# Merging the block inverses of a gated delta rule: neighbouring matmuls on different rows of the array

## The chip, the cores and the metric

The kernel runs on one core of a Trainium2 chip, as one launch. The metric is device time in microseconds, the median of several runs. The core has five engines with instruction queues of their own: TensorE (PE; its weight loads stand in the profile as PEld), VectorE (DVE), ScalarE (ACT), GpSimd (POOL) and SyncE (SP, which issues transfers). Each works through its queue in order; semaphores tie the queues together.

## The reference

Two layers of a mixer run over a context of 256 rows and a sequence of 1024 rows, with a model width of 1024. A projection feeds a convolution branch and a branch of four heads with a gated delta rule, once forward and once backward in time. The part that the change touches solves, for every chunk of time and every head, a triangular system:

```python
lmat = jnp.where(strict, jnp.einsum('bhncd,bhnsd->bhncs', kb, k) * decay, 0.0)
eye = jnp.eye(CHUNK, dtype=jnp.float32)
rhs = jnp.concatenate([v * beta, kb * jnp.exp(g)[..., None]], axis=-1)
sol = lax.linalg.triangular_solve(eye + lmat, rhs, left_side=True, lower=True, unit_diagonal=True)
```

The solutions go into a recurrence over the chunks that carries a 128 by 128 state per head and direction. The two directions are added, normalised and gated, and a last projection with a residual closes the layer.

## The kernel before

The time axis is cut into 10 blocks of 128 rows (`NB`); the kernel's chunk is a whole block. For each head, `head_b1` computes for both directions d and all blocks the triangular matrix of keys against keys (`tt`, line 682) and its inverse, so that the recurrence (`head_rec`) needs only products. The inverse is made in three steps:

1. The four 32 by 32 diagonal blocks of every matrix are inverted on DVE by elimination, 30 steps of two instructions (lines 699 and 701), for all blocks and both directions at once. Two transposes on DVE bring the result into the forms needed as operands, `xn` (named xnat in the profile, line 705) and `xt` (xtr, line 706).
2. Pairs of 32 by 32 inverses are merged into 64 by 64 inverses: for an inverse [[A, 0], [C, D]] the missing quarter is minus D^-1 C A^-1. The first products go to the tile `pu` (line 721), ACT copies them with a minus sign to `u1` (line 729), the second products go to `py` (lines 736 and 739), and ACT copies those to their places (line 748). There are two pairs p in a block: p = 0 lies in partitions 0 to 63, p = 1 in 64 to 127. The call's `tile_position` says which rows and columns of the 128 by 128 array a matmul uses: rows start at 32 or 96 for `pu`, at 0 or 64 for `py`. Of `py` there are three kinds, called (p, "n") and (p, "t") by the operand's form; "n" and "t" of the same p use the same rows and different columns.
3. The two 64 by 64 inverses are merged in the same way into the 128 by 128 inverse, five blocks at a time: first products to `pu2` (line 754, rows 64 to 127 of the array; the prediction calls this "up"), copy to `u2` (line 759), second products to `py2` (line 764 for the forward, 767 for the backward direction, rows 0 to 63; "down"), copy into place (lines 770 and 772). In the forward direction GpSimd clears a quarter of the matrix after "up" (line 757).

`pu`, `py`, `pu2` and `py2` all take their turn in two PSUM buffers of one tag, pb, each one bank; other steps use that tag too. Outputs of p = 0 and p = 1 share a bank, in different partitions.

The order of the work as a whole comes from a plan (`PLAN`) that lists the steps of a layer (A to Z: projections of Q, K, V, Z and of the convolution, head_a, head_b1 as B, head_b2 as D, the recurrence as R, convolution taps as T, and so on), from priorities given by step (`LEAD`), and from a scheduler that sets each engine's order when the program is built. B has a priority that lets its matmuls come ahead of projections as soon as the scheduler thinks that they are ready; the projections (line 369, 24 matmuls for a segment of 256 or 512 columns) fill the pauses in between. So a change in one step may move instructions of other steps.

Of the kernel before, what the change touches and what calls it, by code (L numbers as in the profile page):

```python
# [8 lines left out]
F32 = mybir.dt.float32  # L9
# [15 lines left out]
NB = T // 128  # L25
# [45 lines left out]
def mixer_kernel(ctx: ExitStack, tc: tile.TileContext, xs, cst_d, wada, win, wab, gp_d, wout, fnw, out):  # L71
# [11 lines left out]
    def misc(shape=(128, 512)):  # L83
        return bank("pb", 2, shape)
# [306 lines left out]
    for l in range(DEPTH):  # L391
# [274 lines left out]
        def head_b1(h, kq, hs):  # L666
# [48 lines left out]
                    act.activation(aux[rs_, :, cs_], xt[rs_, NB:2 * NB, :], AF.Copy)  # L715
            for d in range(2):
                pu = misc((128, NB, 32))
                for p in range(2):
                    f_, s_ = slice(64 * p, 64 * p + 32), slice(64 * p + 32, 64 * p + 64)
                    for b in range(NB):  # L720
                        pe.matmul(pu[f_, b, :], lhsT=tt[s_, d, b, f_], rhs=xt[s_, d * NB + b, :], start=True,  # L721
                                  stop=True, tile_position=(64 * p + 32, 64 * p))
                if d == 0:
# [4 lines left out]
                    f_ = slice(64 * p, 64 * p + 32)  # L728
                    act.activation(u1[f_], pu[f_], AF.Copy, scale=-1.0)
                py = misc((128, NB, 32))  # L730
                need = ((0, "n"), (0, "t"), (1, "t")) if d == 0 else ((0, "n"), (1, "n"), (1, "t"))
                for p, w_ in need:
                    f_, s_ = slice(64 * p, 64 * p + 32), slice(64 * p + 32, 64 * p + 64)
                    for b in range(NB):
                        if w_ == "n":
                            pe.matmul(py[s_, b, :], lhsT=u1[f_, b, :], rhs=xn[f_, d * NB + b, :], start=True,
                                      stop=True, tile_position=(64 * p, 64 * p + 32))
                        else:
                            pe.matmul(py[f_, b, :], lhsT=xn[f_, d * NB + b, :], rhs=u1[f_, b, :], start=True,
                                      stop=True, tile_position=(64 * p, 64 * p))  # L740
# [5 lines left out]
                          (aux[64:96, :, 32:64], py[64:96]))  # L746
                for o_, i_ in mv:
                    act.activation(o_, i_, AF.Copy)
                for b0 in range(0, NB, 5):
                    pu2 = misc((64, 5, 64))  # L750
                    for j in range(5):
                        b = b0 + j
                        rhs = tts[0][64:128, b, 64:128] if d == 0 else aux[64:128, b, :]
                        pe.matmul(pu2[:, j, :], lhsT=tt[64:128, d, b, 0:64], rhs=rhs, start=True, stop=True,
                                  tile_position=(64, 0))
                    if d == 0:
                        pool.memset(tts[0][64:128, b0:b0 + 5, 0:64], 0.0)
                    u2 = rwp.tile([64, 5, 64], F32, tag="u1", name="u2", bufs=2)
                    act.activation(u2, pu2, AF.Copy, scale=-1.0)
                    py2 = misc((128, 5, 64))  # L760
                    for j in range(5):
                        b = b0 + j
                        if d == 0:
                            pe.matmul(py2[0:64, j, :], lhsT=aux[0:64, b, :], rhs=u2[:, j, :], start=True, stop=True,
                                      tile_position=(0, 0))
                        else:
                            pe.matmul(py2[64:128, j, :], lhsT=u2[:, j, :], rhs=tts[1][0:64, b, 0:64], start=True,
                                      stop=True, tile_position=(0, 64))
                    if d == 0:
                        act.activation(tts[0][0:64, b0:b0 + 5, 64:128], py2[0:64], AF.Copy)  # L770
                    else:
                        act.activation(tts[1][64:128, b0:b0 + 5, 0:64], py2[64:128], AF.Copy)
            return tts

        def head_b2(h, kq, v, hs):
# [317 lines left out]
```

## Time and profile before

| What | us |
|---|---|
| median of 3 runs | 1629.67 |
| lowest and highest run | 1625.31, 1635.13 |
| profiled execution, own time | 1630.59 |
| its span, first to last instruction | 1628.9 |
| PE busy | 1498.2 |
| DVE busy | 1264.7 |
| ACT busy | 896.5 |
| POOL busy | 147.0 |

The busy time of an engine is the time in which at least one of its instructions was under way. Matmuls are pipelined, so a record of 0.19 us does not mean that the next one starts 0.19 us later: what a group of matmuls costs is read from the start of its first to the start of the next work. A matmul in 4-byte numbers leaves two weight loads and two matmul records. In the timeline neighbouring records of the same kind are merged into one row with a count, and the row's length runs to the end of its last record.

### The profile page before, as it was taken

How to read it: one execution, taken by the hardware profiler on the slowest of the kernel's cores; microseconds unless marked ns; L12 is line 12 of the kernel's file. 1: busy time of each engine (PE TensorE's matmuls, PEld its weight loads, DVE VectorE, ACT ScalarE, POOL GpSimd, SP SyncE). 2: the span in 40 equal slices, each digit the busy share in tenths (PEclk: the TensorE clock that was granted, in tenths of full speed). 3: DMA queues.
4: the chain of work that ended last, by engine and by line, in shares of the span. 5: the costliest groups of instructions: out<-in, count | busy, mean ns of one | idle time of the engine just before them, and what ended most of it. 6: DMA issues, size and time to landing. Idle time of an engine off the chain costs nothing. (4 is left out here: it accounts for less than half of the span.)

```text
span 1628.9 us, 27580 instructions
## 1 busy us (share of the span) xinstructions
PE 1498.2 (92%) x10536; PEld 1029.2 (63%) x10536; DVE 1264.7 (78%) x2813; ACT 896.5 (55%) x2009; POOL 147.0 (9%) x252
## 2 busy tenths in 40 slices
PE   7898899899999998999799999898999999999697
PEld 1564576478556765676577664675575575577576
DVE  3867889988596978876587578889898887877475
ACT  3756466466537563654443465684675666476221
POOL 0002001100111011101000010011011001111000
PEclk9798999999999999999899999999999999999899
DMA  9212102410232123333653131014013201253541
GB/s 303 96 51 104 40 28 82 155 40 27 72 114 91 53 94 98 112 134 131 218 162 113 40 96 60 28 59 133 19 45 118 84 27 72 92 173 106 188 157 70
DMA packets 83264, 158.21 MB, mean 97 GB/s; under 512 B 5606, under 2 KB 52700, under 8 KB 83132
## 3 DMA queue, kind: packets, MB, share of 16 engines
q1 hardware_dynamic: 67344, 96.74, 19.2%
q0 software_dynamic: 15280, 59.52, 10.4%
q8 instruction: 83, 1.36, 0.3%
q14 instruction: 49, 0.40, 0.1%
q10 hardware_dynamic: 508, 0.19, 0.0%
HBM read 125.43 MB, written 30.99 MB: 96 GB/s over the span
## 5 line engine op out<-in xcount | busy, mean ns | idle before, releaser
L369 PE MATMUL pj<-hhi,whi 128*128 128x512 f16 (+1 forms) x1184 | 427.8, 361 | 7.9 <-ACT whi L292 5.3
L369 PE MATMUL pj<-hhi,wlo 128*128 128x512 f16 (+1 forms) x1184 | 428.5, 362 | 2.9 <-DVE wlo L293 2.6
L369 PE MATMUL pj<-hlo,whi 128*128 128x512 f16 (+1 forms) x1184 | 428.2, 362 | 0.0
L369 PEld LDWEIGHTS <-whi 128*128 128x128 f16 x2368 | 233.5, 100 | 183.2 <-issue 18.8
L531 DVE SCALAR_TENSOR_TENSOR acc<-u,cws,acc 128x960 f32<-128x960 f32 (+26 forms) x240 | 228.3, 951 | 2.7 <-ACT acc L514 1.1
L369 PEld LDWEIGHTS <-wlo 128*128 128x128 f16 x1184 | 118.2, 100 | 91.9 <-issue 8.1
L966 PE MATMUL pj<-woh,yh 128*128 128x512 f32 x256 | 102.6, 401 | 9.7 <-ACT yh L959 9.7
L616 DVE SCALAR_TENSOR_TENSOR kq<-raw,cst,kq 128x1284 f32<-128x1284 f32 (+1 forms) x64 | 94.6, 1479 | 14.3 <-ACT kq L614 14.1
L966 PE MATMUL pj<-woh,yl 128*128 128x512 f32 x256 | 101.5, 398 | 4.6 <-DVE yl L960 4.6
L284 ACT ACTIVATE whi<-wst 128x1024 bf16<-128x1024 f32 x56 | 59.1, 1056 | 80.3 <-PE pj L369 72.7
L966 PE MATMUL pj<-wol,yh 128*128 128x512 f32 x256 | 101.8, 398 | 0.0
L833 ACT ACTIVATE vs<-rc,hs 128x128 f32<-128x128 f32 x144 | 52.4, 368 | 66.4 <-PE rc L830 64.5
L699 DVE TENSOR_TENSOR et<-xp 128x30 f32<-128x30 f32 (+14 forms) x240 | 83.8, 349 | 5.7
L701 DVE TENSOR_TENSOR xp<-xp,et 128x30 f32<-128x30 f32 (+14 forms) x240 | 80.6, 336 | 5.5
L292 ACT ACTIVATE whi<-wst,w_s 128x1024 f16<-128x1024 f32 x56 | 64.3, 1148 | 36.9 <-DVE w_s L152 36.0
L293 DVE SCALAR_TENSOR_TENSOR wlo<-wst,w_s,whi 128x1024 f16<-128x1024 f32 x56 | 73.9, 1320 | 12.6 <-ACT whi L292 12.6
L162 PE MATMUL pw<-scond,wst 128*128 128x128 f32 x512 | 68.6, 276 | 0.3 <-DVE md L179 0.3
L162 PEld LDWEIGHTS pw<-scond,wst 128*128 128x128 f32 x512 | 63.0, 191 | 3.4 <-DVE md L179 1.2
L840 PE MATMUL rc<-vs,ktm 128*128 128x128 f32 x288 | 61.7, 301 | 3.7 <-ACT vn L836 3.0
L840 PEld LDWEIGHTS rc<-vs,ktm 128*128 128x128 f32 x288 | 43.8, 190 | 30.3 <-ACT vn L836 25.4
L966 PEld LDWEIGHTS pj<-woh,yh 128*128 128x128 f32 x256 | 49.1, 192 | 20.5 <-ACT yh L959 9.9
L589 ACT ACTIVATE raw<-pj,wm 128x512 f32<-128x512 f32 (+1 forms) x68 | 42.2, 621 | 33.4 <-PE pj L369 24.1
(365 smaller groups left out, 3021.5 us busy)
## 6 DMA issues: line engine op xcount, KB each, us to landing
wst<-in_win_dram SPq DMA_DIRECT2D x56, 512.0 KB, 3.6
row<-rdr POOLq DMA_DIRECT2D x35, 640.0 KB, 4.8
wst<-in_wada_dram SPq DMA_DIRECT2D x32, 512.0 KB, 3.6
x<-in_xs_dram SPq DMA_DIRECT2D x20, 512.0 KB, 7.0
ast<-in_wada_dram SPq DMA_DIRECT2D x8, 1024.0 KB, 10.8
wst<-in_wout_dram SPq DMA_DIRECT2D x16, 512.0 KB, 4.2
y<-ydr SPq DMA_DIRECT2D x18, 448.0 KB, 6.8
a<-cdr SPq DMA_DIRECT2D x9, 512.0 KB
```

Source lines behind the costliest of these rows:

```text
L162: pe.matmul(o, lhsT=w[:, k, :], rhs=scond[:, k:k + 1, :].to_broadcast([128, 64, 2]), start=(k == 0), stop=(k == KT - 1))
L284: act.activation(hi.bitcast(BF16), st, AF.Square, accum_out=ss)
L292: act.activation(hi, st, AF.Identity, scale=s[:, 0:1])
L293: dve.scalar_tensor_tensor(out=lo, in0=st, scalar=s[:, 0:1], in1=hi, op0=MUL, op1=SUB)
L369: pe.matmul(pj[:, 0:n], lhsT=a[:, k, :], rhs=b[:, k, t0:t0 + n], start=(i == 0), stop=(i == 3 * KT - 1))
L531: gates["big"] = dve.scalar_tensor_tensor(out=ao, in0=ui, scalar=cws[:, 0, j:j + 1], in1=ao, op0=MUL, op1=ADD)
L616: gates["big"] = dve.scalar_tensor_tensor(out=dst, in0=src[:, o0 + j:o0 + j + n], scalar=col("sw", j0 + j), in1=dst, op0=MUL, op1=ADD)
L699: dve.tensor_tensor(out=ev, in0=xp[:, j + 1:, j:j + 1].to_broadcast([128, ni, j]), in1=xp[:, j:j + 1, 0:j].to_broadcast([128, ni, j]), op=MUL)
L701: dve.tensor_tensor(out=xp[:, j + 1:, 0:j], in0=xp[:, j + 1:, 0:j], in1=ev, op=ADD)
L833: act.activation(vss[d], pns[d], AF.Identity, scale=hs[:, 2 + d, bs[d]:bs[d] + 1])
L840: pe.matmul(pkv, lhsT=ktm[:, bs[d], :], rhs=vss[d], start=True, stop=True)
L966: pe.matmul(pj[hf], lhsT=a[:, k, :], rhs=w[k][:, hf * 512:(hf + 1) * 512], start=k == 0 and i == 0, stop=k == KT - 1 and i == 2)
```

## The change

`head_b1` issues the same matmuls on the same operands in another order. In `pu` the two pairs p alternate block by block, where all blocks of p = 0 came ahead of all of p = 1. In `py` the three kinds alternate block by block, in an order that puts different rows next to each other. In the last merge the "down" of the first five blocks alternates with the "up" of the other five, and the two copies at the end follow both "down" groups; the tiles `pu2` of the second five and `py2` of the first five are taken ahead of that group. The new local functions `up`, `down` and `turn` stand in the diff.

```diff
--- before.py
+++ after.py
@@ -715,9 +715,10 @@
                     act.activation(aux[rs_, :, cs_], xt[rs_, NB:2 * NB, :], AF.Copy)
             for d in range(2):
                 pu = misc((128, NB, 32))
-                for p in range(2):
-                    f_, s_ = slice(64 * p, 64 * p + 32), slice(64 * p + 32, 64 * p + 64)
-                    for b in range(NB):
+
+                for b in range(NB):
+                    for p in range(2):
+                        f_, s_ = slice(64 * p, 64 * p + 32), slice(64 * p + 32, 64 * p + 64)
                         pe.matmul(pu[f_, b, :], lhsT=tt[s_, d, b, f_], rhs=xt[s_, d * NB + b, :], start=True,
                                   stop=True, tile_position=(64 * p + 32, 64 * p))
                 if d == 0:
@@ -728,10 +729,10 @@
                     f_ = slice(64 * p, 64 * p + 32)
                     act.activation(u1[f_], pu[f_], AF.Copy, scale=-1.0)
                 py = misc((128, NB, 32))
-                need = ((0, "n"), (0, "t"), (1, "t")) if d == 0 else ((0, "n"), (1, "n"), (1, "t"))
-                for p, w_ in need:
-                    f_, s_ = slice(64 * p, 64 * p + 32), slice(64 * p + 32, 64 * p + 64)
-                    for b in range(NB):
+                need = ((0, "n"), (1, "t"), (0, "t")) if d == 0 else ((1, "n"), (0, "n"), (1, "t"))
+                for b in range(NB):
+                    for p, w_ in need:
+                        f_, s_ = slice(64 * p, 64 * p + 32), slice(64 * p + 32, 64 * p + 64)
                         if w_ == "n":
                             pe.matmul(py[s_, b, :], lhsT=u1[f_, b, :], rhs=xn[f_, d * NB + b, :], start=True,
                                       stop=True, tile_position=(64 * p, 64 * p + 32))
@@ -746,30 +747,48 @@
                           (aux[64:96, :, 32:64], py[64:96]))
                 for o_, i_ in mv:
                     act.activation(o_, i_, AF.Copy)
-                for b0 in range(0, NB, 5):
-                    pu2 = misc((64, 5, 64))
-                    for j in range(5):
-                        b = b0 + j
-                        rhs = tts[0][64:128, b, 64:128] if d == 0 else aux[64:128, b, :]
-                        pe.matmul(pu2[:, j, :], lhsT=tt[64:128, d, b, 0:64], rhs=rhs, start=True, stop=True,
-                                  tile_position=(64, 0))
+                u2, pu2, py2 = {}, {}, {}
+
+                def up(b0, j):
+                    b = b0 + j
+                    rhs = tts[0][64:128, b, 64:128] if d == 0 else aux[64:128, b, :]
+                    pe.matmul(pu2[b0][:, j, :], lhsT=tt[64:128, d, b, 0:64], rhs=rhs, start=True, stop=True,
+                              tile_position=(64, 0))
+
+                def down(b0, j):
+                    b = b0 + j
+                    if d == 0:
+                        pe.matmul(py2[b0][0:64, j, :], lhsT=aux[0:64, b, :], rhs=u2[b0][:, j, :], start=True, stop=True,
+                                  tile_position=(0, 0))
+                    else:
+                        pe.matmul(py2[b0][64:128, j, :], lhsT=u2[b0][:, j, :], rhs=tts[1][0:64, b, 0:64], start=True,
+                                  stop=True, tile_position=(0, 64))
+
+                def turn(b0):
                     if d == 0:
                         pool.memset(tts[0][64:128, b0:b0 + 5, 0:64], 0.0)
-                    u2 = rwp.tile([64, 5, 64], F32, tag="u1", name="u2", bufs=2)
-                    act.activation(u2, pu2, AF.Copy, scale=-1.0)
-                    py2 = misc((128, 5, 64))
-                    for j in range(5):
-                        b = b0 + j
-                        if d == 0:
-                            pe.matmul(py2[0:64, j, :], lhsT=aux[0:64, b, :], rhs=u2[:, j, :], start=True, stop=True,
-                                      tile_position=(0, 0))
-                        else:
-                            pe.matmul(py2[64:128, j, :], lhsT=u2[:, j, :], rhs=tts[1][0:64, b, 0:64], start=True,
-                                      stop=True, tile_position=(0, 64))
+                    u2[b0] = rwp.tile([64, 5, 64], F32, tag="u1", name="u2", bufs=2)
+                    act.activation(u2[b0], pu2[b0], AF.Copy, scale=-1.0)
+
+                pu2[0] = misc((64, 5, 64))
+                for j in range(5):
+                    up(0, j)
+                turn(0)
+
+                pu2[5], py2[0] = misc((64, 5, 64)), misc((128, 5, 64))
+                for j in range(5):
+                    down(0, j)
+                    up(5, j)
+                turn(5)
+                py2[5] = misc((128, 5, 64))
+                for j in range(5):
+                    down(5, j)
+                for b0 in (0, 5):
+                    py2_ = py2[b0]
                     if d == 0:
-                        act.activation(tts[0][0:64, b0:b0 + 5, 64:128], py2[0:64], AF.Copy)
+                        act.activation(tts[0][0:64, b0:b0 + 5, 64:128], py2_[0:64], AF.Copy)
                     else:
-                        act.activation(tts[1][64:128, b0:b0 + 5, 0:64], py2[64:128], AF.Copy)
+                        act.activation(tts[1][64:128, b0:b0 + 5, 0:64], py2_[64:128], AF.Copy)
             return tts
 
         def head_b2(h, kq, v, hs):
```

What the scheduler makes of it is shown at three places of PE's order.

The first is on PE in the first head, forward direction, at the second products `py` (pb in the rows; u is the copied first product, xnat one form of the 32 by 32 inverses; whi, wlo, hhi and hlo belong to a projection). Before:

```order
L369 LDWEIGHTS whi
L369 MATMUL pj<-hlo,whi 128x512
L736 MATMUL pb<-xnat,u_1849 32x32 x10
L739 MATMUL pb<-u_1849,xnat 32x32 x20
L369 LDWEIGHTS wlo
L369 MATMUL pj<-hhi,wlo 128x512
```

and with the change:

```order
L369 MATMUL pj<-hlo,whi 128x512
L737 MATMUL pb<-xnat,u_1849 32x32
L369 LDWEIGHTS wlo
L369 MATMUL pj<-hhi,wlo 128x512
L369 LDWEIGHTS whi
L369 MATMUL pj<-hhi,whi 128x512
L740 MATMUL pb<-u_1849,xnat 32x32 x2
L737 MATMUL pb<-xnat,u_1849 32x32
L740 MATMUL pb<-u_1849,xnat 32x32 x2
L737 MATMUL pb<-xnat,u_1849 32x32
```

The thirty matmuls alternate now, and two matmuls of a projection have come between the first and the rest.

The second is on PE in the same head and direction, in the last merge, where "down" of the first five blocks (L764, then L761) meets "up" of the other five (L754, then L755). Before:

```order
L369 LDWEIGHTS whi
L369 MATMUL pj<-hlo,whi 128x512
L764 MATMUL pb<-u_1893,aux 64x64 x5
L754 MATMUL pb<-tt 64x64 x5
L369 LDWEIGHTS wlo
```

and with the change:

```order
L761 MATMUL pb<-u_1893,aux 64x64
L755 MATMUL pb<-tt 64x64
L761 MATMUL pb<-u_1893,aux 64x64
L755 MATMUL pb<-tt 64x64
L761 MATMUL pb<-u_1893,aux 64x64
L755 MATMUL pb<-tt 64x64
L761 MATMUL pb<-u_1893,aux 64x64
L755 MATMUL pb<-tt 64x64
L761 MATMUL pb<-u_1893,aux 64x64
L755 MATMUL pb<-tt 64x64
```

The two groups of five, next to each other already, alternate matmul by matmul.

The third is on PE ahead of the second head's first products (L721, then L722), with the numbers of the tiles, since the rows read alike without; pj_3348 is a segment of a convolution projection with the weights 2713, pj_3321 and pj_3375 are segments of another with the weights 3183. Before:

```order
L369 LDWEIGHTS wlo_2755
L369 MATMUL pj_3348<-hhi_82,wlo_2755 128x512
L369 LDWEIGHTS whi_3183
L369 MATMUL pj_3375<-hhi_82,whi_3183 128x512
L721 MATMUL pb_3000<-xtr_2985,tt_2864 32x32 x20
L369 LDWEIGHTS whi_3183
```

and with the change:

```order
L369 MATMUL pj_3321<-hhi_82,whi_3183 128x512
L369 LDWEIGHTS whi_3183
L369 MATMUL pj_3321<-hlo_83,whi_3183 128x512
L369 LDWEIGHTS wlo_3190
L369 MATMUL pj_3321<-hhi_82,wlo_3190 128x512
L369 LDWEIGHTS whi_2713
L369 MATMUL pj_3348<-hhi_82,whi_2713 128x512
L722 MATMUL pb_3000<-xtr_2985,tt_2864 32x32 x20
```

The segment pj_3348 had been finished ahead of that group and is only begun there now.

## Rows read from the trace of the kernel before

**Rows 1.** The page's head: span, then busy time of each engine.

```profile
span 1628.9 us, 27580 instructions
...
PE 1498.2 (92%) x10536; PEld 1029.2 (63%) x10536; DVE 1264.7 (78%) x2813; ACT 896.5 (55%) x2009; POOL 147.0 (9%) x252
```

**Rows 2.** Table by stretches, columns: stretch, length, busy us of PE, PEld, DVE, ACT, POOL.

```profile
327.00:470.00 143.00, 137.87 (x1093) 98.03 (x1093) 111.40 (x229) 80.89 (x190) 7.82 (x14) 0.98 0.17 56
...
1277.00:1405.50 128.50, 121.72 (x918) 78.79 (x919) 108.59 (x230) 78.77 (x180) 9.09 (x15) 0.99 0.16 56
```

**Rows 3.** Chain that ended last, 1277 to 1310, shares by engine and line.

```profile
by line: PE pj L369 40.7%; PE pb L721 8.7%; PE pb L783 8.2%; PE pb L754 8.1%; PE pa L167 6.8%; PE pw L162 6.6%; PE pb L736 5.6%; DVE xtr L706 5.4%; PE pb L739 5.3%; PE pb L767 4.3%; PE pb L764 4.0%; PE pb L803 1.0%; issue 0.4%; PE pw L290 0
```

**Rows 4.** The same chain, 1373 to 1405.

```profile
by line: DVE et L699 27.8%; DVE xp L701 25.9%; issue 14.6%; DVE xp L694 6.3%; DVE xtr L706 5.9%; DVE wlo L293 4.0%; DVE sgz L596 4.0%; ACT xg L689 2.3%; DVE u L502 2.2%; PE pj L369 1.4%; DVE wm L298 1.2%; DVE ost L142 1.0%; PE pa L876 0.8%;
```

**Rows 5.** Waits of PE: us in total, times, longest.

```profile
PE pb L721 <- DVE xtr L706: 22.3, 7, 4.4
...
PE pb L721 <- DVE ost L872: 2.7, 1, 2.7
```

**Rows 6.** Timeline of PE at 181: start, us, engine, line, instruction, count, idle.

```profile
181.00 1.35 PE L721 MATMUL pb<-xtr,tt 32*32 32x32 f32 x40 [3.33 <-DVE xtr L706]
182.28 0.39 PE L369 MATMUL pj<-hlo,whi 128*128 128x256 f16 x1
```

**Rows 7.** Timeline of PE at 188, second products, first direction of the first head.

```profile
187.92 0.72 PE L736 MATMUL pb<-xnat,u 32*32 32x32 f32 x17
188.46 0.21 PE L739 MATMUL pb<-u,xnat 32*32 32x32 f32 x1
188.48 0.19 PE L736 MATMUL pb<-xnat,u 32*32 32x32 f32 x1
188.51 0.19 PE L739 MATMUL pb<-u,xnat 32*32 32x32 f32 x1
...
189.74 0.39 PE L369 MATMUL pj<-hhi,wlo 128*128 128x512 f16 x1
```

**Rows 8.** Timeline of PE at 191 to 194, the 64 by 64 groups.

```profile
191.29 0.76 PE L754 MATMUL pb<-tt 64*64 64x64 f32 x10
191.99 0.39 PE L369 MATMUL pj<-hhi,wlo 128*128 128x512 f16 x1
192.21 0.38 PE L369 MATMUL pj<-hhi,whi 128*128 128x512 f16 x1
...
192.83 0.62 PE L764 MATMUL pb<-u,aux 64*64 64x64 f32 x7
193.24 0.27 PE L754 MATMUL pb<-tt 64*64 64x64 f32 x1
...
193.96 0.39 PE L369 MATMUL pj<-hhi,wlo 128*128 128x512 f16 x1
```

**Rows 9.** Timeline of PE at 71, gate projection.

```profile
71.34 0.17 PE L431 MATMUL pb<-gw,hlo 128*128 128x16 f16 x1
...
71.59 0.18 PE L429 MATMUL pb<-gw,hhi 128*128 128x32 f16 x1
```

**Rows 10.** Timeline of PE at 344 to 346, second head, other direction.

```profile
344.15 0.81 PE L736 MATMUL pb<-xnat,u 32*32 32x32 f32 x20
344.90 0.28 PE L369 MATMUL pj<-hlo,whi 128*128 128x256 f16 x1
345.11 0.72 PE L736 MATMUL pb<-xnat,u 32*32 32x32 f32 x17
...
346.39 0.28 PE L369 MATMUL pj<-hhi,wlo 128*128 128x256 f16 x1
```

**Rows 11.** Timeline of ACT at 1284.

```profile
1284.74 0.43 ACT L748 ACTIVATE aux<-pb 32x320 f32<-32x320 f32 x1 [3.10 <-PE pb L739]
```

**Rows 12.** Timeline of PE at 327, second head.

```profile
326.94 2.15 PE L721 MATMUL pb<-xtr,tt 32*32 32x32 f32 x40 [4.21 <-DVE xtr L706]
329.03 0.61 PE L369 MATMUL pj<-hlo,whi 128*128 128x512 f16 x1
```

## The prediction

> **What bounds the kernel now.** I read the page first: TensorE (PE) is busy 1498.2 us of 1628.9, VectorE (DVE) 1264.7 us [rows 1]. Neither is idle for long, so the next view is the table by stretches, cut where the first merge group of each head starts (8 heads: 4 in each of 2 layers). In two such stretches PE is busy 137.87 of 143 us and 121.72 of 128.5; DVE 111.40 and 108.59 [rows 2]. So PE is nearly full, and DVE is the second bound.
>
> The chain shows how they alternate. From 1277 to 1310, the merges of one head, it runs on PE almost alone [rows 3]; the other items there are projections that fill the pauses between merge groups. From 1373 to 1405, the elimination of the next head, it runs on DVE, and ends with the transpose `xtr` [rows 4]. PE then waits for that transpose before the first merge group: 22.3 us in 7 heads, and 2.7 us in the eighth for another DVE instruction [rows 5]. A microsecond saved on PE in a merge is thus on the path where it is saved, but a head later the elimination on DVE may take it back. PE's total alone does not tell the gain.
>
> **What a merge group costs now.** A matmul in 4-byte numbers leaves two records, called passes here. All of it repeats in both directions of 8 heads, 16 times.
>
> - First products, `pu`: 20 matmuls, 40 passes. The group starts at 181.00 and the next work at 182.28: 1.28 us [rows 6].
> - Second products, `py`: 30 matmuls, 60 passes, from 187.92 to 189.74: 1.81 us [rows 7]. The first 17 passes take 0.72 us, of which the last alone lasts 0.19; with a longer first step that is 32 to 33 ns from start to start.
> - 64 by 64, "up": 5 matmuls, 10 passes, 191.29 to 191.99: 0.70 us, and 58 to 60 ns from start to start ((0.76-0.22)/9 = 60) [rows 8].
> - 64 by 64, "down" of the first five blocks and "up" of the other five, one behind the other: 192.83 to 193.96, 1.13 us [rows 8].
>
> What two tiles of the array do at once can be seen where one run of matmuls hands over to the next. At 188.46 a pass of L739 starts while four of L736 are still to come or just begun, and for 0.1 us both lines start a pass every 32 ns, each at its own pace: 188.46 and 188.51 for L739, 188.48 between them for L736 [rows 7]. At 193.24 the same happens between L764 (rows 0 to 63 of the array) and L754 (rows 64 to 127) [rows 8]. So matmuls on different tiles do overlap and the second does not slow the first; in the order of before it lasts for a few passes only, since the next row group is ten or twenty passes away.
>
> **The change, part by part.** (1) Alternating `pu`. Without any other limit, two streams of 20 passes would need 20 times 32 ns, 0.64 us. But PE has to be handed the instructions too. The densest stretch of the trace that lasts is the gate projection: from 71.34 to 71.59 ten matmuls, each with its weight load, start 25 ns apart, with 16 and with 32 columns alike [rows 9]. The handover at 188.46 is denser, but there the passes were already queued. The two bounds for a pass are therefore 16 ns (the handover's pace) and 25 ns; above them stands 32 ns, no gain. I take 25: it is the only pace here that holds over many matmuls, although with other operands. Then `pu` takes 39 x 0.025 + 0.12 (the time from its last start to the next work, 182.28 - 181.00 - 1.16) = 1.10 us: 0.18 saved. At 16 ns it would be 0.50.
>
> (2) `py` by the same pace: 59 x 0.025 = 1.48 us between first and last start, where it was 1.81 - 0.12 = 1.69: 0.21 saved. Its three products lie on three tiles, two of them on the same rows; the handover from L736 to L739 at 188.46 was between just those two, so same rows with other columns do not exclude overlap. If all three ran abreast, 60 passes would need 20 x 32 = 0.64 us: 1.03 saved (0.65 to stay on the safe side of first-pass delays).
>
> (3) Middle 64 by 64 group: at 58 ns a pass the 25 ns floor does not bind. Ten passes of each stream side by side take what one takes alone, 0.70 us, plus a few hundredths: 0.75 against 1.13, 0.38 saved. The lone "up" at the start and "down" at the end stay as they are.
>
> (4) Splits. In the forward direction the second matmul of `py` now needs the second half of `u1`, which ScalarE (ACT) copies last. The order answers with a split: one matmul, a few projections, then the other 29. There are seven such splits where there was one. The trace has one: 344.15 to 344.90 and 345.11 to 346.39, 0.75 + 1.28 = 2.03 against 1.81 us for a whole group, 0.22 each [rows 10]. Six more cost 1.3 us.
>
> (5) ACT's copies. They might have started on the half that was ready first, and interleaving makes all halves ready last. But in the trace they start only when the whole group is over: the first copy of `py` at 1284.74 after a wait of 3.10 us for L739, though its operand comes from the first run, L736 [rows 11]. So nothing is lost there, and a shorter group lets them start earlier. GpSimd's (POOL's) clears of the merged quarters wait for the same groups as before; PSUM buffers turn over in the same order, with two in use at a time.
>
> (6) A projection changes places. Between the first groups of the first and the second head the order has 387 projection matmuls in 16 bits before and 363 after: 24 of them, one segment of a convolution projection, now come behind the second head's first group. At their pace of 0.22 us (191.99, 192.21) [rows 8] that is 5.2 us. PE already waits 4.21 us in front of that group [rows 12], so it arrives earlier for nothing, and the stretch behind it, where PE is busy 137.87 of 143 us, gets 5.2 us more; its end has 2.7 us of PE waiting [rows 5] to take up a part. I count 2.5 us lost; bounds 0 and 5.2. DVE's set of instructions between these points does not change by more than a few short ones.
>
> **The sum.** PE saves 16 x (0.18 + 0.21 + 0.38) = 12.3 us, less 1.3 for splits: 11.0. Of this I let 60% arrive: in the stretch from 1277 to 1405.5 the merge and its tail (33 us) are PE's, the last 32 us are DVE's, and DVE is busy 108.59 of 128.5 us. 6.6 us gained, less 2.5 for the moved projection: 4.1. The profiled execution took 1630.59 us, its span 1628.9; the median of the three runs, 1629.67, is within 0.1% of it. 1630.6 - 4.1 = 1626.5, rounded to **1626**.
>
> A rule of the Trainium skill speaks against parts 1 and 2. TensorEngine Tiling (Array Packing), "Restrictions and Gotchas", says that different row tiles cannot access the same PSUM bank at the same time; `pu` and `py` each lie in one bank. By that rule only the middle group, whose two outputs lie in two buffers, would gain. The trace disagrees where it can: 60 passes of `py` at 32 ns would take 1.92 us between first and last start, and with two handovers they take 1.69, so both overlap, the one between two row groups as well as the one between two column groups.
>
> **The rivals.** *No floor at 25 ns.* For it: the handover's pace. Against it: it never lasts. Then PE saves 16 x (0.50 + 0.65 to 1.03 + 0.38) = 24 to 31 us, less 1.3; 60% of it is 14 to 18, less 2.5: about **1617**, down to 1615. The Trainium skill's page "TensorE: Matmul & The Clock Gate", Part 3, "The mechanism", shows matmuls on different row groups starting some 4 ns apart, which would be this case; no stretch of this trace holds such a pace.
>
> *Alternation does not pay in the 32 by 32 groups* (each change of tile costs what the overlap gives, or one bank serves one row group). Then 16 x 0.38 - 1.3 = 4.8, 60% of it 2.9, less 2.5: **1630**, no change.
>
> *Slower: the elimination swallows it.* PE reaches each first group earlier, DVE does not, and PE only waits longer. The price is the moved segment in full, 5.2 us, and a slower PE behind longer waits: after 4.21 us of idling the second head's first group takes 329.03 - 326.94 = 2.09 us where the first head's takes 1.28 [rows 6, 12], about what the lower of the clock's two levels, 1.2 and 2.4 GHz, makes of it. One such loss of 0.8 us more in three heads, 2.5, with 1.3 for splits: 1630.6 + 5.2 + 2.5 + 1.3 = **1639.6**. It decides if the transposes `xtr` come no earlier than before, counted from the merge ahead of them.
>
> **How the numbers follow.** Forecast (25 ns, partly arriving) 0.50; no floor 0.22; no gain in the small groups 0.15; swallowed 0.13. The order moves many other instructions by a few places, which I take as some 6 us either way around each case. A measurement of this kernel tells about 0.5%, 8 us, from no change. Faster by more: most of the second case (0.19) and about a third of the first (0.16): 0.35. Slower by more: 0.07 of the last case, 0.03 from the scatter of the first and 0.02 from the third: 0.12. The rest, 0.53, is within 0.5%. The range of 8 in 10 runs from the no-floor case to just short of the swallowed one: 1612 to 1638.
>
> **What would show it.** In the profile of the changed kernel: neighbours in `pu` 25 ns apart and the group 1.10 us (0.7 without a floor, 1.28 without overlap); `py` about 1.6 us to the next work; the middle group 0.75 us; PE's wait for `xtr` grown from 22.3 us by several us, above all at the second head. If the groups shrink as said and the time does not move, part 6 and the elimination took it; if they shrink to half, the floor was wrong; if the whole gets slower with short groups, the moved order is the cause.

## The result and the profile after

The changed kernel takes 1611.32 us (median of four runs, 1609.66 to 1614.86) beside 1629.87 for the kernel before (1625.31 to 1635.13): a ratio of 0.9875, 95% interval 0.9845 to 0.9904, about 20 us faster. (The medians lie 18.6 us apart. Ratios, and the gains in us taken from them below, are not quotients of medians; the two differ by up to some 2 us.) That is just below the low end of the predicted range (1612) and 15 us below the predicted time. The profiled execution took 1614.86 us.

The page's head, as in [rows 1]:

```profile
span 1612.9 us, 27598 instructions
...
PE 1471.7 (91%) x10536; PEld 998.6 (62%) x10536; DVE 1265.0 (78%) x2813; ACT 897.5 (56%) x2009; POOL 144.4 (9%) x252
```

The same matmuls keep PE busy 26.5 us less; DVE and ACT did not change. The timeline of PE at the first head, as in [rows 6] (start, us, engine, line, instruction, count, idle before):

```profile
182.22 0.82 PE L722 MATMUL pb<-xtr,tt 32*32 32x32 f32 x40 [3.33 <-DVE xtr L706]
182.97 0.28 PE L369 MATMUL pj<-hlo,whi 128*128 128x256 f16 x1
```

The group `pu` goes from 1.28 to 0.75 us. In `py` of the other direction, the counterpart of [rows 7], all three kinds run abreast:

```profile
198.12 0.22 PE L737 MATMUL pb<-xnat,u 32*32 32x32 f32 x2
198.13 0.21 PE L740 MATMUL pb<-u,xnat 32*32 32x32 f32 x1
198.17 0.20 PE L737 MATMUL pb<-xnat,u 32*32 32x32 f32 x2
198.18 0.19 PE L740 MATMUL pb<-u,xnat 32*32 32x32 f32 x1
...
198.75 0.19 PE L740 MATMUL pb<-u,xnat 32*32 32x32 f32 x1
198.88 0.39 PE L369 MATMUL pj<-hlo,whi 128*128 128x512 f16 x1
```

Sixty passes start between 198.12 and 198.75, 10.7 ns apart on the mean (0.63/59), in rounds of three every 32 ns; the group takes 0.76 us where [rows 7] has 1.81. The middle 64 by 64 group, as in [rows 8], "down" and "up" in pairs:

```profile
201.84 0.27 PE L764 MATMUL pb<-tt,u 64*64 64x64 f32 x1
201.84 0.27 PE L755 MATMUL pb<-aux,tt 64*64 64x64 f32 x1
201.94 0.22 PE L764 MATMUL pb<-tt,u 64*64 64x64 f32 x1
201.95 0.22 PE L755 MATMUL pb<-aux,tt 64*64 64x64 f32 x1
...
202.57 0.39 PE L369 MATMUL pj<-hlo,whi 128*128 128x512 f16 x1
```

It takes 0.73 us, was 1.13 (in two of the sixteen such groups 0.94 and 1.09). Waits of PE (us in total, times, longest), as in [rows 5]:

```profile
PE pb L722 <- DVE xtr L706: 20.8, 7, 4.6
...
PE rc L872 <- DVE row L816: 3.0, 1, 3.0
PE pb L722 <- DVE ost L891: 2.7, 1, 2.7
```

The wait for the transposes did not grow (25.0 us before, 23.5 after, with the one for ost); a wait of 3.0 for L816 is new.

**One measure for all runs.** For every merge group of a trace I take the time from its first start to the start of the next work on PE, and add them up. Before: 96.1 us. After: 63.0. So the merges give PE 33.1 us back, three times the 11.0 of the prediction's sum. That is more than by the rows above, since groups at the lower clock, which take twice as long, shrink too, and in these traces three first groups instead of four lie at it as a whole (granted clock 0.50).

### The profile page after: what moved, and what is told of

It reads as the page before. It is cut to its first block, busy times and chain, and to the rows that moved or that the text cites. A ratio compares the mean times of both kernels' runs of the same rounds, so it can differ in the third digit from the quotient of the medians.

```text
span 1612.9 us, 27598 instructions
## 1 busy us (share of the span) xinstructions
PE 1471.7 (91%) x10536; PEld 998.6 (62%) x10536; DVE 1265.0 (78%) x2813; ACT 897.5 (56%) x2009; POOL 144.4 (9%) x252
## 5 line engine op out<-in xcount | busy, mean ns | idle before, releaser
L369 PE MATMUL pj<-hhi,whi 128*128 128x512 f16 (+1 forms) x1184 | 427.0, 361 | 11.1 <-DVE sgz L596 5.2
L369 PE MATMUL pj<-hhi,wlo 128*128 128x512 f16 (+1 forms) x1184 | 425.7, 360 | 3.8 <-DVE wlo L293 3.8
L369 PE MATMUL pj<-hlo,whi 128*128 128x512 f16 (+1 forms) x1184 | 427.1, 361 | 0.0
L369 PEld LDWEIGHTS <-whi 128*128 128x128 f16 x2368 | 232.3, 100 | 187.0 <-issue 22.8
L369 PEld LDWEIGHTS <-wlo 128*128 128x128 f16 x1184 | 118.1, 100 | 93.1 <-DVE wlo L293 7.6
L845 DVE SCALAR_TENSOR_TENSOR bv<-rc,hs,bv 128x128 f32<-128x128 f32 x144 | 48.1, 347 | 18.2 <-PE rc L844 15.4
```

The source lines that it names most:

```text
L369: pe.matmul(pj[:, 0:n], lhsT=a[:, k, :], rhs=b[:, k, t0:t0 + n], start=(i == 0), stop=(i == 3 * KT - 1))
```

## The experiments

Two questions. First, what is the pace of matmuls on different tiles: does each tile keep its own (theory), or can PE start none sooner than 25 ns after the last (the prediction's choice)? Second, 33 us less on PE gave 20 us: does a fixed share arrive, or does all of it arrive and the new order of the other engines' work cost something (theory O)? Each run stands against the kernel before on the same chip.

### One edit at a time, in the order of before

Only `pu` by turns; the order of all other engines' instructions is that of before.

```diff
-                for p in range(2):
-                    f_, s_ = slice(64 * p, 64 * p + 32), slice(64 * p + 32, 64 * p + 64)
-                    for b in range(NB):
+                for b in range(NB):
+                    for p in range(2):
+                        f_, s_ = slice(64 * p, 64 * p + 32), slice(64 * p + 32, 64 * p + 64)
                         pe.matmul(pu[f_, b, :], ...
```

> The kernel before with one part of the change alone: the first products pu alternate between the two pairs. Every engine's order outside these groups is word for word that of the kernel before. Theory 'overlap': the group takes 0.75 us as in the changed kernel and not 1.28 (1.2 and not 2.1 where the clock is low), PE saves 16 x 0.53 = 8.5 us or a little more, and somewhat over half of it arrives, as of the whole change (18.6 of 33): 1624 to 1626, ratio 0.996 to 0.998. Rival 'order' (the new order of the other instructions brings the gain): groups shorter, time as before, ratio 0.999 to 1.001.

Measured: 0.992 (0.9898 to 0.9941), 13 us faster. The merge groups take 87.0 us, 9.1 less: 0.57 per group, not 0.18. The rival is out; the theory's own ratio (0.996 at best) lies outside the interval too, for more time came than PE was freed of.

In the second run `pu` is as before, and in `py` the two kinds of one pair, which use the same rows and different columns, alternate:

```diff
-                for p, w_ in need:
+                pairs = (((0, "n"), (0, "t")), ((1, "t"),)) if d == 0 else (((0, "n"),), ((1, "n"), (1, "t")))
+                for p, w_, b in [(p, w_, b) for pr in pairs for b in range(NB) for p, w_ in pr]:
```

> The kernel before with another part alone, in a form that keeps the order of all other engines: in the second products py only the two kinds on the same rows and different columns alternate, the third kind stays a run by itself. Theory 'any two tiles overlap': the group of 60 passes falls from 1.81 to about 1.3 us (two runs of 20 at 32 ns), PE saves 16 x 0.5 = 8 us, ratio 0.995 to 0.998. Rival 'only different rows overlap': the group stays at 1.8 us, ratio 0.999 to 1.001.

Measured: 0.9929 (0.9905 to 0.9952), 12 us faster; merge groups 87.5 us, 8.6 less. Its timeline of PE:

```profile
187.72 0.21 PE L737 MATMUL pb<-xnat,u 32*32 32x32 f32 x1
187.72 0.21 PE L740 MATMUL pb<-u,xnat 32*32 32x32 f32 x1
187.77 0.19 PE L737 MATMUL pb<-xnat,u 32*32 32x32 f32 x1
187.78 0.19 PE L740 MATMUL pb<-u,xnat 32*32 32x32 f32 x1
```

Behind the first pass both kinds start every 32 ns, up to 10 ns apart, and the group takes 1.29 us (187.72 to the next work at 189.00). Different columns are enough for two matmuls to overlap; the rows need not differ.

### The new order without the overlap

The order of the changed kernel on the other engines, but within the merge groups runs of one tile again:

```diff
-                for b in range(NB):
-                    for p in range(2):
+                for p in range(2):
+                    for b in range(NB):
...
+                turns = [(0, w) for w in need] + [(b, w) for w in need for b in range(1, NB)]
...
+                for f, b0, j in ((down, 0, 0), (down, 0, 1), (down, 0, 2), (down, 0, 3), (up, 5, 0), ...
```

> The changed kernel with its own order on all other engines, kept word for word, but inside the merge groups runs of the same tile: pu by pairs, py by kinds after the first matmul of each kind, the middle group in runs of four. Theory 'overlap': the groups are nearly as long as before (pu 1.28, py 1.7 to 1.8, middle 0.9 to 1.0 us), PE loses some 27 of the 33 us again, and the time goes back to 1624 to 1632. Rival 'order': the time stays at 1610 to 1616.

Measured: 1.0008 (0.999 to 1.0026). The new order alone brings nothing in sum, and the rival 'order' is out. The merge groups still took 90.8 us, 5.3 less, from the handovers that are left; that these 5.3 us did not show in the time is the first sign that the new order costs something.

### The pace by itself

Matmuls of 32 by 32 between two other steps, each kind in a loop of its own (r is the first row of the tile in the array, the next argument its first column, the last says 16 bits), written to a PSUM tile that nobody reads; the rest is the changed kernel.

```diff
+                pe.matmul(**one(o, j, 0, 0, False))
+            for j in range(16):
+                for r in (0, 32):
+                    pe.matmul(**one(o, j, r, r + 32, False))
...
+                for r in (0, 32, 64, 96):
+                    pe.matmul(**one(o, j, r, r, True))
```

> The changed kernel with test matmuls of 32 by 32 put in once behind the gate values of the first layer: in 4 bytes 16 on one tile, 32 on two tiles of different rows, 32 on two tiles of the same rows, 64 on four tiles; in 16 bits 16 on one tile and 64 on four tiles. Theory 'each tile its own pace, no floor': 32, 16, 16 and 8 ns from pass to pass; in 16 bits below 25 ns on one tile. Rival 'a matmul can be handed over every 10.6 ns at best', the pace of py in the changed kernel: 32, 16, 16 and 10.6. If the 25 ns of the gate projection are a floor for matmuls with 16-bit operands, both patterns of these stand at 25.

Timeline of PE, lines 491 (one tile), 498 (two tiles, same rows), 502 (four tiles), 505 and 509 (16 bits: one tile, four tiles); then a table of two stretches with the granted clock in the third column from the right:

```profile
90.87 1.10 PE L491 MATMUL pb<-gg 32*32 32x32 f32 x29
...
93.82 1.92 PE L498 MATMUL pb<-gg 32*32 32x32 f32 x64
95.67 0.61 PE L369 MATMUL pj<-hhi,wlo 128*128 128x512 f16 x1
96.21 1.71 PE L502 MATMUL pb<-gg 32*32 32x32 f32 x110
...
98.47 0.50 PE L505 MATMUL pb<-hhi,gw 32*32 32x32 f16 x13
...
98.85 0.70 PE L509 MATMUL pb<-hhi,gw 32*32 32x32 f16 x60
```

```profile
90.90:92.30 1.40, 1.40 (x65) 1.40 (x66) 1.40 (x3) 0.00 (x0) 0.00 (x0) 1.00 0.72 257
92.40:99.50 7.10, 6.84 (x313) 5.67 (x307) 2.83 (x7) 0.87 (x4) 0.00 (x0) 0.50 0.02 5
```

One tile at the full clock, 2.4 GHz: (1.10 - 0.19)/28 = 32.5 ns a pass. From 92.4 on the granted clock is 0.50, the level of 1.2 GHz, so the later lines are slow in themselves; even so two tiles on the same rows take (1.92 - 0.24)/63 = 27 ns a pass, and four tiles (1.71 - 0.24)/109 = 13.5 ns (what is taken off is the length of one pass). In 16 bits one tile takes (0.50 - 0.18)/12 = 27 ns, four tiles (0.70 - 0.18)/59 = 8.8 ns a pass. At this clock neither the 8 ns that the theory expected of four tiles in 4 bytes nor less than 25 ns on one tile in 16 bits could be seen, and no run shows them at the full clock. But 8.8 ns rules out both the floor of 25 ns and the rival's 10.6. So the 25 ns of [rows 9] cannot have been the pace at which PE is handed instructions. They would fit the pace of one stretch of array that every matmul there uses, as one tile in 16 bits takes 27 ns here; at the full clock that was not tried.

### Adding up in the order of before

The first two edits together; the order of the other engines is that of before.

> pu by turns and, in py, the two kinds of one pair (same rows, other columns) by turns, as the two runs before did one at a time; the order of DVE, ACT, POOL and SP is that of before, instruction for instruction. The merge groups should occupy PE 96.1 - 9.1 - 8.6 = 78.4 us. Theory O (overlap is worth more than 100% of what it takes off PE, and the new order of the changed kernel costs part of it): the two gains add up, 12.4 + 11.5 = 24 us, ratio 0.985, no worse than the changed kernel, which takes 33 us off PE instead of 18. Theory S (about 56% of any PE time saved arrives, and the two single gains were generous by chance): 17.7 x 0.56 = 10 us, ratio 0.994.

Measured: 0.9887 (0.9866 to 0.9907), 18.5 us (15.2 to 21.9) for 17.4 us of PE (groups 78.7). In sum all of it arrives: half of the changed kernel's PE gain brings nearly its whole time gain. Both theories' numbers miss the interval, 0.994 (S) by far and 0.985 (O), for the two single gains did not add up in full.

Then "down" and "up" overlap by two blocks as well, with the copy of the first half ahead of the second "down":

```diff
+                for j in range(3):
+                    down(0, j)
+                for j in range(2):
+                    down(0, 3 + j)
+                    up(5, j)
+                for j in range(3):
+                    up(5, 2 + j)
+                evac(0)
```

> As the run before it, and down of the first five blocks overlaps up of the second five by two blocks, with the copy of the first half straight behind; the order of the other engines then differs from before in a few places only (60 rows of DVE against 1138 in the changed kernel). Theory O: as the run before it and about 3 us less, ratio 0.983. Theory S: 12 us, 0.993. If the early copies or the wait for the second down lose, it is above the run before it.

Measured: 0.9875 (0.9848 to 0.9902), 20.4 us for 19.7 us of PE. From the run before it the intervals cannot tell it apart; 0.993 (S) and 0.983 (O) both lie outside.

The changed kernel beside them:

> The changed kernel on this chip, beside the others: 0.9875 by its own measurement (0.9845 to 0.9904). Both theories expect that; it is there to set the others against.

Measured: 0.9855 (0.9831 to 0.9879), 23.7 us for 33.0 us of PE (groups 63.1).

The last run here has `pu` by turns and all three kinds of `py` by turns, without the change to the 64 by 64 groups; its scheduler result is a third order:

```diff
-                for p, w_ in need:
+                turns = [(p, w_, b) for b in range(NB) for p, w_ in need]
+                for p, w_, b in turns:
```

> pu by turns and py's three kinds by turns, one pass of each, in the order of the kinds that before has; the 64x64 group stays as before. Only these; the other engines' order then moves of itself, at other places than in the changed kernel (1152 rows of DVE differ from it). PE occupation about 96.1 - 9.1 - 17 = 70 us. Theory S: 26 x 0.56 = 14.6 us, 0.991. Theory O: the overlap alone is worth up to 30 us (0.982), minus what this third order costs or plus what it gains; if it comes out near e5 though it saves 8 us more on PE, the order decides over the rest.

Measured: 0.99 (0.9876 to 0.9924), 16.3 us for 21.8 us of PE (groups 74.3). It frees 4.4 us more of PE than the fifth run (e5 in the expectation) and is no faster, so time does not follow PE's gain alone. It does not decide between the theories: S named 0.991, O left open what a third order costs. In its trace the stretch behind the last head's first merges is the longest of all, 130.1 us against 117.7 in the fifth run.

### Mixing the orders by head

Where does the changed kernel's order cost time? Cut by heads' first merge groups, its trace was longer than that of the fifth run in two places: from the first to the third head (285.8 and 288.2 us in its two traces above, against 283.2), where a projection segment was moved, and behind the last head's first merges (124.3 and 123.2 against 117.7). The form of the fifth run keeps the order of before, head by head, so it can be put in just there:

```diff
+FULL = [(0, 2), (0, 3), (1, 0), (1, 1), (1, 2)]
...
+                full = (l, h) in FULL
+                if full:
+                    need = ((0, "n"), (1, "t"), (0, "t")) if d == 0 else ((1, "n"), (0, "n"), (1, "t"))
+                    pairs = (need,)
+                else:
+                    pairs = (((0, "n"), (0, "t")), ((1, "t"),)) if d == 0 else (((0, "n"),), ((1, "n"), (1, "t")))
...
+                if not full:
+                    for b0 in range(0, NB, 5):
...
+                    continue
```

> The changed kernel, but three of the eight heads (the first two of the first layer and the last of the second) have pu by turns, py's two kinds of one pair by turns and the 64x64 group as before, which gives these heads the order of before on the other engines; the remaining five have the changed code and the changed order. By theory O (the new order costs time in just these places) the stretches should be those of the run with that form in the first two heads (283 us from the first to the third head's merges, against 286 to 288 in the changed kernel) and in the last (118 against 123 to 124), and those of the changed kernel elsewhere: 8 to 10 us less than the changed kernel, about 1602, ratio 0.981. Rival F (the order does not matter, PE time saved does): three heads give back 2 us of PE each, 56% of it arrives: 3 us slower than the changed kernel, 0.988.

Measured: 0.9823 (0.9799 to 0.9848), median 1603.45 us: 28.9 us for 29.2 us of PE. It is the fastest, 7.5 us below the changed kernel on the same chip (1610.96), although PE has 3.9 us more to do in the merges. Rival F is out, and the two stretches came out as expected, 283.3 and 117.7 us.

But the new order does not only cost. Between the first merges of the third and of the fifth head all traces do the same 3489 matmuls (give or take two at the edges). Here are that stretch before, in the fifth run (overlap, order of before), in the third (new order, little overlap) and in this one (stretch, length, busy us of PE, PEld, DVE, ACT, POOL, granted clock, DMA share, GB/s):

```profile
470.00:1023.60 553.60, 515.28 (x3489) 364.45 (x3489) 418.28 (x997) 293.63 (x651) 55.18 (x90) 0.97 0.34 108
```

```profile
464.50:1018.20 553.70, 517.89 (x3489) 365.86 (x3489) 420.16 (x997) 293.40 (x651) 55.77 (x90) 0.96 0.33 108
```

```profile
475.30:1018.50 543.20, 512.74 (x3489) 362.51 (x3489) 417.69 (x998) 294.06 (x652) 53.41 (x90) 0.98 0.33 110
```

```profile
464.20:1006.80 542.60, 506.22 (x3489) 355.46 (x3489) 417.79 (x997) 294.03 (x651) 53.62 (x90) 0.98 0.34 111
```

In all five traces with the order of before it takes 553.6 to 555.6 us, in all eight with the changed order 542.6 to 545.9. So the new order is worth some 10 us there, and the overlap nothing in either order. One part of it is a wait of PE for ACT's copy to `aux` between the third and the fourth head, 3.9 us before (start, us, engine, line, instruction, count, idle; the granted clock is 0.51 in the group behind it) and 4.9 in the fifth run:

```profile
496.23 1.32 PE L754 MATMUL pb<-aux,tt 64*64 64x64 f32 x10 [3.89 <-ACT aux L748]
```

In the third run it is gone; the rest of the 10 us I have not traced. That 28.9 us arrived for 29.2 is therefore partly chance: some 10 of them are the order's.

In the last head alone:

> The changed kernel with that smaller form in the last head of the second layer alone; the order of DVE is that of the changed kernel up to that head's transposes and that of before behind them. Theory O: the tail has 118 us instead of 123 to 124, PE's wait of 3 us for the row work in it is gone: 1605 to 1606, ratio 0.983. Rival F: 1 us slower than the changed kernel, 0.987. Rival P (the tail's length hangs on the moment at which it starts, not on its order): anything between.

Measured: 0.9847 (0.9823 to 0.9872), median 1605.99, 5.0 us below the changed kernel. The two intervals overlap, and rival F's 0.987 lies just inside this one, so the time alone does not settle it; the traces say more. The tail, first of the changed kernel, then of this run (columns as above):

```profile
1385.00:1509.20 124.20, 107.88 (x862) 73.43 (x862) 87.74 (x194) 75.72 (x174) 16.25 (x27) 0.94 0.36 123
```

```profile
1382.50:1499.40 116.90, 104.82 (x862) 74.06 (x862) 86.70 (x194) 74.36 (x174) 16.46 (x27) 0.97 0.39 131
```

The same number of matmuls, 7.3 us shorter: PE is busy 3.1 us less, with the clock at 0.97 instead of 0.94, and idle 4.2 us less. (Against the changed kernel's trace on this chip, 122.2 us at a clock of 0.96, it is 5.3 us shorter.) The place is the recurrence of that head. In the changed kernel PE stands still for 3 us there, and just behind it the granted clock falls to 0.50 (from 1423.2 to 1426.5), a projection starting every 0.43 us instead of 0.22:

```profile
1419.16 0.39 PE L873 MATMUL rc<-na,vn 128*128 128x128 f32 x2
1422.53 0.49 PE L872 MATMUL rc<-row,S 128*128 128x128 f32 x2 [2.99 <-DVE row L816]
...
1424.69 0.63 PE L369 MATMUL pj<-hhi,wlo 128*128 128x512 f16 x1
1425.12 0.63 PE L369 MATMUL pj<-hhi,whi 128*128 128x512 f16 x1
```

In this run (L369, 872 and 873 are here L371, 905 and 906) projections lie at that place:

```profile
1417.43 0.39 PE L906 MATMUL rc<-na,vn 128*128 128x128 f32 x2
1417.66 0.38 PE L371 MATMUL pj<-hlo,whi 128*128 128x512 f16 x1
...
1420.46 0.38 PE L371 MATMUL pj<-hhi,wlo 128*128 128x512 f16 x1
1420.68 0.38 PE L905 MATMUL rc<-row,S 128*128 128x128 f32 x2
```

The traces of the other runs agree. The wait of 3 us for L816 or its counterpart stands in all six traces with the changed order in the last head and in no other. With that order the tail takes 122.2 to 124.3 us in five traces and 126.1 without the overlap; with the order of before it takes 116.9 to 118.6 in five traces with some overlap and 119.8 without. One trace does not fit: in that of the sixth run, whose DVE order there is that of before, it has 124.2 us, with a wait of PE of 2.1 us for another step. It is by far the slowest execution of that run (1622.69 us, the others 1607.62 to 1612.44), so the order of DVE does not fix the tail in every execution.

The first two heads alone:

> The changed kernel with the smaller form in the first two heads of the first layer alone; that puts the 24 projection matmuls back behind the first head's merges (387 and 407 of them in the first two stretches, where the changed kernel has 363 and 431). Part 6 of the prediction: the moved segment costs 2.5 us (0 to 5.2), of which the smaller overlap gives back 4 us of PE, 2.3 of time: no change against the changed kernel or up to 3 us faster, 0.984 to 0.986. If the move cost nothing, 2.3 us slower than it, 0.987 to 0.988.

Measured: 0.986 (0.9836 to 0.9883), median 1609.61: 1.4 us below the changed kernel, within what was expected for a segment that costs 2.5 us, but too little to be told from no effect. The stretch itself is clearer; the changed kernel first, then this run:

```profile
182.20:468.00 285.80, 266.01 (x2155) 183.38 (x2156) 244.11 (x491) 166.92 (x399) 23.70 (x37) 0.98 0.21 67
```

```profile
179.00:463.00 284.00, 266.71 (x2156) 187.19 (x2156) 242.84 (x491) 166.84 (x399) 23.08 (x37) 0.99 0.21 68
```

It is 1.8 us shorter, and 4.4 against the third trace of the changed kernel (288.4), although the merge groups of the trace take PE 3.7 us more, 2.9 of it here.

And the changed kernel beside them:

> The changed kernel on the same chip as the three mixed ones, to set them against: 0.9855 to 0.9875.

Measured: 0.9868 (0.9845 to 0.9891), 21.5 us for 33.1 us of PE.

## Why the prediction was right and wrong

**The floor of 25 ns (parts 1 and 2) is the step that failed.** I had two paces, 16 ns from the handover in [rows 7] and 25 ns from [rows 9], and took 25 because it lasts. But ten matmuls on the whole array, one behind the other, show only how fast one piece of the array takes them. The handover was the right row, since it alone had several tiles at work, and the runs show the rest: at the full clock each tile of the array starts a 32 by 32 pass in 4 bytes every 32 ns, with one, two or three tiles at work. So `pu` saved 0.53 us, not 0.18; `py` 1.05 where it is not split, not 0.21. The rival without a floor named these (0.50; 0.65 to 1.03) and its time, 1617 down to 1615, was the nearest; I gave it 0.22 when its mechanism was the one at work. It was still 4 to 6 us too high (with 0.65 its own terms give 1619, not 1617): it took `py` from 0.65 on, and had no term for the groups at the lower clock.

**Part 3 holds:** 0.40 us, 0.38 said. **Part 4 holds:** `py` is split seven times, where it was once. The lone first matmul takes 0.18 us (187.12 to 187.30) and the other 58 passes 0.76 us (187.83 to 188.59), as long as 60 do elsewhere: 0.18 a split, where 0.22 was said.

```profile
187.12 0.24 PE L737 MATMUL pb<-xnat,u 32*32 32x32 f32 x2
187.30 0.39 PE L369 MATMUL pj<-hhi,wlo 128*128 128x512 f16 x1
```

**Part 5 holds.** ACT's first copy of `py` waited 3.10 us in [rows 11]; at the same head it now starts 1.58 us after the last copy to `u1` ends (1262.76 + 0.88 to 1265.22), and does not start late:

```profile
1262.76 0.88 ACT L730 ACTIVATE u<-pb 32x320 f32<-32x320 f32 x2
...
1265.22 0.43 ACT L749 ACTIVATE aux<-pb 32x320 f32<-32x320 f32 x1
```

**"60% arrives" had the right number by luck.** 20.4 of 33.1 us is 62%; over the three measurements of the changed kernel it is 62, 72 and 65%. I had put the loss down to the elimination on DVE, which would take PE's gain back as a longer wait for `xtr`. That wait did not grow: 22.3 us before, 19.3 to 22.5 in every other trace. This also ends the slower rival. Nor is there a fixed share. With the order of before kept, the whole gain arrives in sum (18.5 for 17.4, 20.4 for 19.7). With the changed order kept, from the third run to the changed kernel, the merges give back 27.8 us and the time falls by 22 to 25 (from a ratio of 1.0008 to 0.9855 to 0.9875). Within each of these sums nothing arrives between the third and the fifth head, and elsewhere between four fifths of what is freed and more than all of it. Why it is so much elsewhere I have not shown.

What the new order is worth is nothing in sum (1.0008), but not in its parts. By the traces of the kernel before and of the third run, stretch by stretch, it costs 4.2 us from the first to the third head, gains 10.4 to the fifth, gains 1.6 to the last, and costs 7.5 behind the last head's first merges. So the 11 us by which the changed kernel falls short of the 33 are not simply the price of its order; by the traces they are mostly what does not arrive between the third and the fifth head, and what the order costs in two places, less what it gains in the others.

**Part 6 was right in kind and too small.** It priced the moved segment at 2.5 us. The run with the old form in the first two heads is 1.8 to 4.4 us shorter there, with 2.9 us more of merges in the stretch, and the new order without the overlap is 4.2 us longer there than before (289.0 and 293.2); all of these are the order of two whole heads, and no run moves the segment alone. And I looked only at the first two heads: for the tail of the second layer, where the order costs most by the traces (a wait of 3 us that no projection fills, and a lower clock behind it), and for the stretch where it gains, I had listed no term.

**The rival of the shared bank** falls. By the trace passes of `pu` and `py` with different rows and outputs in one PSUM bank run abreast: `pu` in 0.75 us, where its 40 passes one behind the other take 1.28. The rule in the Trainium skill, TensorEngine Tiling (Array Packing), "Restrictions and Gotchas", that different row tiles cannot access one bank at the same time, does not hold here in that form; the outputs lie in different partitions of the bank, which may be the difference, and the same partitions were not tried. What the Trainium skill shows in "TensorE: Matmul & The Clock Gate", Part 3, "The mechanism", starts some 4 ns apart on different row groups, is borne out in kind: neighbours start 10 ns apart or less in the rows above (198.12 and 198.13).

## What to carry to other kernels

The pace of small matmuls belongs to the tile of the array, so look for rows in which several tiles work, however short, and do not take one tile's pace for a limit of the engine. After an edit that reorders, split the gain in two: what the engine's groups give back, and what the new order of everything else costs or gains, stretch by stretch and not in sum. Here an edit with half the gain in the old order was about as fast, and taking each order where it is good (by head) beat both. Where the gain is less than the engine gave back, look for new waits of a few microseconds, and at the granted clock behind them.

## What was not expected of the hardware

- Two tiles on the same rows of the array and different columns overlap as fully as two on different rows: `py` went from 1.81 to 1.29 us by that alone, and to 0.76 with the third kind.
- Sixty passes in 0.63 us, 10.7 ns from start to start, and in 16 bits four tiles 8.8 ns at the lower clock: one tile at 32 ns, or two, do not show how fast the engine can start matmuls.
- Behind a wait of PE of 3 us the granted clock went to its lower level (0.50 from 1423.2 to 1426.5), and the projections there started twice as far apart (0.43 us instead of 0.22).
